# Small norm operations on GpSimd, and mixed channels loaded once for the second output projection

## The chip, the cores and the metric

The kernel runs on one core of a Trainium2 chip, as a single program. The metric is the time of one execution on the device in microseconds; of several runs the median is given. A profiled execution has its own time, which stands beside its span below.

The core has a matrix engine (TensorE, PE in the profile; PEld is its loading of weights), VectorE (DVE), ScalarE (ACT) and GpSimd (POOL). SyncE (SP) computes nothing here; most DMAs are issued from its queue. Each engine works through its own queue in order.

## The reference

One layer of a hybrid encoder on 2048 tokens of 1024 channels, then a final RMSNorm. Cut to what matters:

```python
h = rmsnorm(x, norm_mix_g)
u, dq, dk, dv, cq, cf, ci, cg = split_projection(h @ w_in)
y_a = s5_mixer(u, ...)                      # 256 channels
y_b = diff_attention(dq, dk, dv, ...)       # 6 heads x 64 channels
y_c = hgrn2_mixer(cq, cf, ci, cg, ...)      # 6 heads x 64 channels, the recurrence
x = x + concatenate([y_a, y_b, y_c]) @ w_out
h = rmsnorm(x, norm_ffn_g)
x = x + (gelu(causal_conv3(h @ w_up) + conv_b) * (h @ w_gate)) @ w_down
out = rmsnorm(x, final_norm_g)
```

Two of the norms matter here. In attention each head's output `o` (two softmax maps, subtracted and multiplied by `v`) goes through `rmsnorm(o, subln_g)` over its 64 channels. In the recurrence each head's `o` goes through `rmsnorm(o, norm_g)`, and is then multiplied by `silu(g)`. A norm needs, for every token and head, one reciprocal square root.

## The kernel before, in words

Products are made of f16 pairs: a float32 value is split into a high and a low half (`Ctx.split`, L52: ACT writes the high half at L55, DVE the low half at L61 or L63, or POOL at L59), and one product takes three matmuls. Tokens are tiled in four chunks of 512 (`CH`), channels in tiles of 128.

The program has two strands, `left` and `right` (L2050, L2061), that a function `weave` (L2084) interleaves by weights while the program is written down. The left strand projects to queries, keys and values and then runs attention in two passes: query blocks 0 to 7 for all six heads, then blocks 8 to 15. The right strand runs the S5 group, then the recurrence (`phase_hgrn`), then the tail (`phase_tail`). The order that each engine finally gets is made when the program is built: the context is opened with `schedule_with_timeline_sim=True` (L2131), so that a planner orders the instructions by a simulated time, and a change of one instruction's engine can move others.

**Attention's norms.** `phase_attn` (L754) collects, for each head `h` and pass, the sums of squares of its outputs in `H.ss` and the softmax sums in `H.la`, as tiles `[128, 8]` (128 tokens, 8 query blocks). When the last block of a head has been put away, `norm(h)` (L923) makes the factors: a reciprocal (L927), then on DVE two products (L928, L929), a scale with an added epsilon (L930), the reciprocal square root `K.rsqrt`, and a product (L934); POOL then multiplies the head's output by them (L935). After an odd head the pair is transposed by the PE (L944), split, and written to `Yd`, the mixed channels in DRAM (L948). There are 12 such norms.

**The reciprocal square root** (`Ctx.rsqrt`, L67): POOL raises to the power -0.5 (L72), and one step of Newton's method follows on DVE: L75, L84 and L85 for these two norms (n is 8).

**The recurrence's norms.** `phase_hgrn` (L1011) goes through 12 units (three pairs of heads by four chunks), each in the steps `proj`, `pre` and `fin`. In `fin` (L1290) ACT squares the output (L1335), DVE sums (L1337), scales and adds epsilon on DVE (L1340), calls `rsqrt` (L1343), lets POOL multiply by the gate (L1345), and multiplies on DVE by the factors (L1347).

**The output projection in two parts.** Chunks 0 and 1 are projected beside the recurrence (`early_mix`, L1375). Chunks 2 and 3 are projected in `second` (L1960) by `project` (L1467), between the down projection of the first MLP half and the second MLP half. `project` makes the columns in two halves `n`, and for each half goes through four groups `q` of 256 mixed channels. For each `n` and `q` it loads the mixed channels (`o_y`, two DMAs of 256 KB from `Yd`, L1478) and the weights in float32 (`o_wst`, 512 KB, L1480), splits the weights (`o_w`), and issues 24 matmuls (L1493). The channels do not depend on `n`, so they are loaded twice for each chunk. Their ring has 2 tiles, that of the split weights 3 and that of the raw weights 2 (L1967). `put` adds the product to the residual (`o_r`, L1506) and ACT makes sums of squares (`f_sq`, L1594). Between the two halves of chunk 3, chunk 2 is transposed for the MLP (`turned`, L1531). In the same stretch the last parts of the down projection run: raw weights `f_dst` are loaded (L1713) and combined on POOL and DVE (L1863), split into `f_dw`, and multiplied (`f_pd`, L1786); finished rows leave through L1608 and L1612.

Of the kernel before, what the change touches and what calls it, by code (L numbers as in the profile page):

```python
# [10 lines left out]
F16 = mybir.dt.float16  # L11
# [3 lines left out]
ALU = mybir.AluOpType  # L15
# [11 lines left out]
CH = 512  # L27
# [11 lines left out]
class Ctx:  # L39
# [24 lines left out]
                out=lo, in0=src, scalar=scale, in1=hi, op0=ALU.mult, op1=ALU.subtract  # L64
            )

    def rsqrt(self, pool, v, n, tag):  # L67

        nc = self.nc
        y = pool.tile([128, n], F32, tag=tag + "y", name="rs_y")  # L70
        t = pool.tile([128, n], F32, tag=tag + "t", name="rs_t")
        nc.gpsimd.tensor_tensor(  # L72
            out=y, in0=v, in1=self.mhalf.to_broadcast([128, n]), op=ALU.pow
        )
        nc.vector.scalar_tensor_tensor(  # L75
            out=t, in0=y, scalar=v[:, 0:1] if n == 1 else -0.5, in1=y, op0=ALU.mult, op1=ALU.mult
        )
        if n == 1:
            nc.vector.tensor_scalar(
                out=t, in0=t, scalar1=-0.5, scalar2=1.5, op0=ALU.mult, op1=ALU.add  # L80
            )
            nc.vector.tensor_tensor(out=y, in0=y, in1=t, op=ALU.mult)
        else:
            nc.vector.tensor_tensor(out=t, in0=t, in1=v, op=ALU.mult)  # L84
            nc.vector.scalar_tensor_tensor(  # L85
                out=y, in0=t, scalar=1.5, in1=y, op0=ALU.add, op1=ALU.mult
            )
        return y
# [665 lines left out]
def phase_attn(K, A, QKd, Vd, Yd, i0, i1, s_bufs, lean):  # L754
# [5 lines left out]
    tc, nc = K.tc, K.nc  # L760
    V = nc.vector
    NT = i1 - i0
    LM = 128 * i1
    base, nlam, lk, gc = A.base, A.nlam, A.lk, A.gc
    with ExitStack() as es:
        kp = es.enter_context(tc.tile_pool(name="t_k", bufs=2, reuse_waits="tile"))
        sp = es.enter_context(tc.tile_pool(name="t_s", bufs=s_bufs, reuse_waits="tile"))
        wp = es.enter_context(tc.tile_pool(name="t_w", bufs=2 if lean else 3, reuse_waits="tile"))
        mp = es.enter_context(tc.tile_pool(name="t_m", bufs=3, reuse_waits="tile"))
        op = es.enter_context(tc.tile_pool(name="t_o", bufs=2, reuse_waits="tile"))  # L770
# [152 lines left out]
        def norm(h):  # L923

            H = heads[h]
            s, v = [mp.tile([128, NT], F32, tag=f"e{j}", name=f"t_e{j}") for j in range(2)]
            V.reciprocal(out=s, in_=H.la[:, 0, :])  # L927
            V.tensor_tensor(out=v, in0=s, in1=s, op=ALU.mult)  # L928
            V.tensor_tensor(out=v, in0=v, in1=H.ss, op=ALU.mult)  # L929
            V.tensor_scalar(  # L930
                out=v, in0=v, scalar1=1.0 / HD, scalar2=EPS, op0=ALU.mult, op1=ALU.add
            )
            r = K.rsqrt(mp, v, NT, "rs")
            V.tensor_tensor(out=s, in0=s, in1=r, op=ALU.mult)  # L934
            nc.gpsimd.tensor_tensor(  # L935
                out=H.o, in0=H.o, in1=s.rearrange("p (t o) -> p t o", o=1).to_broadcast([128, NT, HD]),
                op=ALU.mult,
            )
            if h % 2 == 0:
                return  # L940
            for j in range(NT // 4):
                pt = ps_s.tile([128, 512], F32, tag="s", name="t_pt")
                for b in range(4):
                    nc.tensor.transpose(pt[:, 128 * b:128 * b + 128], H.y[:, 4 * j + b, :], K.ident)  # L944
                o = op.tile([128, 2, CH], F16, tag="yo", bufs=1, name="t_yo")
                K.split(o[:, 0, :], o[:, 1, :], pt, gc[:, 0:1])
                c0 = 128 * i0 + j * CH
                nc.sync.dma_start(out=Yd[2 + h // 2, :, :, c0:c0 + CH], in_=o)  # L948
            K.pairs.append(h // 2)
# [30 lines left out]
        for h in range(NH):  # L980
# [5 lines left out]
            for i in range(i0, i1):  # L986
# [10 lines left out]
                t = (h, i, [])  # L997
                n = 2 * (i // 4 + 1)
# [12 lines left out]
def phase_hgrn(K, Hd, w_in, lb_logits, norm_g, Yd, spare):  # L1011
# [5 lines left out]
    tc, nc = K.tc, K.nc  # L1017
    V = nc.vector
    C0 = 1408
    NB = CH // 128  # L1020
    with ExitStack() as es:
# [4 lines left out]
        wp = pool("g_w", 1)  # L1026
        st = pool("g_st", 1)
        hp = pool("g_h", 2)
        w3 = pool("g_3", 3)
        w2 = pool("g_2", 2)  # L1030
# [11 lines left out]
        for hl in (32, 16, 8):  # L1042
            m = ones[:, 0:64].rearrange("p (b y) -> p b y", y=hl)
            nb = 64 // hl
            t = w2.tile([128, nb, hl], F32, tag="d", name="g_mk")
# [11 lines left out]
        t = w2.tile([128, 16, 8], F32, tag="d", name="g_mk2")  # L1057
# [232 lines left out]
        def fin(u):  # L1290

            pr, j = divmod(u, NCH)
            vn, sg, qh, kt, eb, sc = ready.pop(u)
            po = [pp.tile([128, NB, HD], F32, tag="g", name=f"g_ps{a}") for a in range(2)]
            for bk in range(NB):
                for a in range(2):
                    rows = slice(64 * a, 64 * a + 64)
                    for e in range(2):
                        hh = slice(64 * e, 64 * e + 64)
                        nc.tensor.matmul(  # L1300
                            out=po[a][hh, bk, :], lhsT=kt[rows, bk, hh], rhs=vn[rows, bk, hh],
                            start=True, stop=True,
                        )
            sts = w2.tile([128, 2 * NB, HD], F32, tag="st", name="g_st")
            states = [state.get(u - 1, zero) if j else zero]
            for wn in range(2 * NB):
                last = 64 * wn + 63
                V.scalar_tensor_tensor(
                    out=sts[:, wn, :], in0=states[-1], scalar=eb[:, last:last + 1],
                    in1=po[wn % 2][:, wn // 2, :], op0=ALU.mult, op1=ALU.add,  # L1310
                )
                states.append(sts[:, wn, :])
            state[u] = states[-1]
            yield 1
            po = [pp.tile([128, NB, HD], F32, tag="g", name=f"g_po{e}") for e in range(2)]
            for bk in range(NB):
                for e in range(2):
                    nc.tensor.matmul(
                        out=po[e][:, bk, :], lhsT=sc[:, e, bk, :],
                        rhs=vn[:, bk, 64 * e:64 * e + 64], start=(bk == 0), stop=False,  # L1320
                    )
            for wn in range(2 * NB):
                bk, a = wn // 2, wn % 2
                for e in range(2):
                    hh = slice(64 * e, 64 * e + 64)
                    nc.tensor.matmul(
                        out=po[e][64 * a:64 * a + 64, bk, :], lhsT=qh[hh, 64 * wn:64 * wn + 64],
                        rhs=states[wn][hh, :], start=False, stop=(bk == NB - 1),
                    )
            sq = w2.tile([128, NB, 2, HD], F32, tag="d", name="g_sq")  # L1330
            y = w2.tile([128, NB, 2, HD], F32, tag="y", name="g_y")
            for e in range(2):
                nc.scalar.copy(y[:, :, e, :], po[e])
            yield 1
            nc.scalar.activation(out=sq, in_=y, func=AF.Square)  # L1335
            ss = w2.tile([128, 2 * NB], F32, tag="ss", name="g_ss")
            V.tensor_reduce(  # L1337
                out=ss, in_=sq.rearrange("p b e d -> p (b e) d"), axis=AX.X, op=ALU.add
            )
            V.tensor_scalar(  # L1340
                out=ss, in0=ss, scalar1=SQ * SQ / HD, scalar2=EPS, op0=ALU.mult, op1=ALU.add
            )
            r = K.rsqrt(w2, ss, 2 * NB, "rs")  # L1343
            yv = y.rearrange("p b e d -> p b (e d)")
            nc.gpsimd.tensor_tensor(out=yv, in0=yv, in1=sg, op=ALU.mult)  # L1345
            yb = y.rearrange("p b e d -> p (b e) d")
            V.tensor_tensor(  # L1347
                out=yb, in0=yb,
                in1=r.rearrange("p (t o) -> p t o", o=1).to_broadcast([128, 2 * NB, HD]),
                op=ALU.mult,  # L1350
            )
            yield 1
            pt = pp.tile([128, CH], F32, tag="g", name="g_py")
            for bk in range(NB):
                nc.tensor.transpose(pt[:, 128 * bk:128 * bk + 128], yv[:, bk, :], K.ident)
            o = w2.tile([128, 2, CH], F16, tag="d", name="g_yo")
            K.split(o[:, 0, :], o[:, 1, :], pt, gc[:, 0:1])
            nc.sync.dma_start(out=Yd[5 + pr, :, :, j * CH:(j + 1) * CH], in_=o)
            yield 1
# [67 lines left out]
def phase_tail(K, x, Xd, ss, Yd, Ad, w_out, norm_g, W, conv_w, conv_b, w_down, final_g, out, es,  # L1427
# [6 lines left out]
    V = nc.vector  # L1434
# [32 lines left out]
    def project(j, qs, st, wp, yp, pms, put, behind=None, between=()):  # L1467


        for n in range(2):  # L1470
            if n == 1:
                yield from between
            cc = slice(512 * n, 512 * n + 512)
            ps = [pms[n % len(pms)].tile([128, 512], F32, tag="m", name="o_pm") for t in range(4)]
            for q in qs:
                y = yp.tile([128, 2, 2, CH], F16, tag="y", name="o_y")
                for k in range(2):
                    nc.sync.dma_start(out=y[:, k], in_=Yd[2 * q + k, :, :, j * CH:(j + 1) * CH])  # L1478
                f = st.tile([128, 2, 512], F32, tag="wst", name="o_wst")
                d = nc.sync.dma_start(  # L1480
                    out=f, in_=w_out[0, 256 * q:256 * q + 256, cc].rearrange("(k p) f -> p k f", p=128)
# [478 lines left out]
    def second(pool, pm, before):  # L1960
# [3 lines left out]
        with ExitStack() as e3:  # L1964
            pool = pooler(e3)
            pm2 = pool("f_pm2", 4, space=PSUM)
            yp, wp, st = pool("o_y2", 2, "left"), pool("f_w2", 3, "left"), pool("f_st2", 2, "left")  # L1967
            fp, xp, rp = pool("f_f2", 2, "left"), pool("f_x", 1, "left"), pool("f_r4", 8, "left")
            left, right = sinks(hc, fp, 3, 2)
            r2, r3 = [], []  # L1970
# [164 lines left out]
```

## Time and profile before

| what | value |
|---|---|
| median of 3 runs | 2719.52 us (2718.45 to 2723.11) |
| the profiled execution's own time | 2723.9 us |
| its span in the profile | 2722.1 us |
| mean granted clock of the PE | 0.934 |
| bytes by DMA | 473.07 MB, 174 GB/s in the mean |

An engine's busy time is a sum over stages that have different limits, so it has to be read by stage. Attention's first pass lies beside S5's end and the recurrence, up to about 1080 us; its second pass lies beside the first MLP half and the start of that half's down projection, up to about 1920 us; the second output projection takes from about 1935 to 2073 us; the second MLP half and its down projection fill the rest. In the rows, `L96` means line 96, `A<-B` names the tile written and the tiles read, and `xN` counts instructions. The rings of tiles show as waits of the engine or queue that wants the next tile.

### The profile page before, as it was taken

The numbers are of one execution on the slowest core, as the hardware profiler recorded it, in microseconds if no ns is written. First come the engines' busy times: TensorE is split into PE (matmuls) and PEld (weight loads), VectorE is DVE, ScalarE is ACT, GpSimd is POOL, SyncE is SP. The second block draws the span as 40 slices with busy tenths as digits, with TensorE's granted clock in tenths as the row PEclk, the third lists the DMA queues.
The fourth block names the chain that finished last, engine by engine and source line by source line (L and its number), as shares of the span: only waits on it lengthen the run. The fifth ranks groups of instructions, "written<-read, shape, count | busy, mean of one in ns | idle before, by whom it ended". The sixth has DMA issues, their size and how long they took to land.

```text
span 2722.1 us, 42584 instructions
## 1 busy us (share of the span) xinstructions
PE 2408.0 (88%) x15438; PEld 1354.2 (50%) x15438; DVE 1873.5 (69%) x3401; ACT 1316.9 (48%) x2470; POOL 1350.7 (50%) x1149
## 2 busy tenths in 40 slices
PE   5998898888888889769988898598979999999998
PEld 4655556766766764334443444243434444444444
DVE  7467756688869885597788998865455655545565
ACT  6333344667757663564466766633235433333321
POOL 5688612455444542367677677515313344444280
PEclk8899898888989989879999999699989999999999
DMA  7676555467456666655466665688784655554733
GB/s 240 230 214 207 167 161 126 94 133 143 104 125 137 132 135 177 161 122 182 150 182 169 183 173 170 207 276 256 266 312 148 204 168 154 155 148 136 286 99 123
DMA packets 556740, 473.07 MB, mean 174 GB/s; under 512 B 277297, under 2 KB 433265, under 8 KB 555505
## 3 DMA queue, kind: packets, MB, share of 16 engines
q1 hardware_dynamic: 534352, 429.97, 56.0%
q10 hardware_dynamic: 22176, 40.38, 4.0%
q8 instruction: 121, 1.98, 0.3%
q14 instruction: 91, 0.74, 0.1%
HBM read 290.35 MB, written 125.83 MB: 153 GB/s over the span
## 4 chain that ended last, share of the span: by engine, by line
PE 22%; DVE 15%; issue 8%; POOL 7%; ACT 7%; DMA 6%; SPq 1%; ACTq 0%; DVEq 0%; POOLq 0%
PE f_pd L1786 10%; PE f_pm L96 7%; POOL f_k L1863 2%; DVE f_a L61 2%; DMA f_dst<-in_w_down_dram 2%; DVE t_sc L836 2%; DVE f_t L1617 2%; PE o_pm L1493 2%; PE o_pe L1411 2%; DVE t_sc L867 1%; DVE f_w L63 1%; POOL f_u L1863 1%; ACT f_t L1615 1%; ACT f_t L1910 1%; ACT t_sc L848 1%
## 5 line engine op out<-in xcount | busy, mean ns | idle before, releaser
L96 PE MATMUL f_pm<-f_q,f_w 128*128 128x512 f16 x3696 | 836.8, 386 | 30.0 <-DVE f_u L1863 9.2
L96 PEld LDWEIGHTS <-f_w 128*128 128x128 f16 x3696 | 363.3, 99 | 487.5 <-issue 70.1
L1786 PE MATMUL f_pd<-f_dw,f_da 128*128 128x512 f16 x1848 | 407.1, 382 | 2.7 <-DVE f_r L1764 1.5
L891 POOL TENSOR_TENSOR t_sc<-t_sc 128x1024 f16<-128x1024 f32 (+7 forms) x144 | 250.6, 1753 | 302.3 <-ACT t_sc L890 279.1
L1786 PEld LDWEIGHTS <-f_da 128*128 128x128 f16 x1848 | 181.1, 98 | 226.2 <-issue 14.5
L832 PE MATMUL t_ps<-t_k,t_q 96*128 96x512 f16 (+2 forms) x480 | 165.9, 372 | 94.6 <-DVE t_mx L836 80.2
L848 ACT ACTIVATE t_sc<-t_sc,t_nm 128x128 f32<-128x128 f32 (+7 forms) x192 | 230.5, 1201 | 6.6 <-DVE f_a L61 1.1
L836 DVE CUSTOM_DVE_ANT_0 t_sc<-t_ps,t_base,t_mx 128x512 f32<-128x512 f32 (+3 forms) x288 | 185.2, 643 | 18.9 <-PE t_ps L832 10.8
L61 DVE TENSOR_TENSOR f_a<-f_t,f_a 128x512 f16<-128x512 f32 x132 | 154.8, 1192 | 48.3 <-ACT f_a L55 47.8
L913 PEld LDWEIGHTS <-t_wt 128*128 128x128 f16 x2448 | 106.3, 101 | 121.3 <-DMA t_wt<-t_sc 50.4
L867 DVE SCALAR_TENSOR_TENSOR t_sc<-t_sc,t_a 128x1024 f32<-128x1024 f32 (+7 forms) x144 | 164.6, 1169 | 1.6
L96 PE MATMUL g_pq<-g_h,g_w 128*128 128x256 f16 x1152 | 159.2, 299 | 5.1 <-DVE g_sg L1160 2.7
L1863 POOL TENSOR_TENSOR f_t<-f_t,f_t 128x512 f32<-128x512 f32 x66 | 101.6, 1553 | 123.1 <-ACT f_a L55 108.8
L913 PE MATMUL t_po<-t_v,t_wt 128*128 128x64 f16 x2448 | 120.5, 198 | 47.2 <-DMA t_wt<-t_sc 42.4
L96 PE MATMUL g_pv<-g_w,g_h 128*128 128x256 f16 x1152 | 150.3, 288 | 9.2 <-ACT g_w L55 9.2
L1863 POOL TENSOR_TENSOR f_k<-f_k,f_k 128x512 f32<-128x512 f32 x88 | 124.5, 1414 | 51.5 <-ACT f_halo L1907 25.4
L1617 DVE SCALAR_TENSOR_TENSOR f_t<-f_u,f_cw,f_t 128x1024 f32<-128x1024 f32 x88 | 124.1, 1410 | 33.1 <-ACT f_t L1615 32.3
L836 DVE CUSTOM_DVE_ANT_0 t_sc<-t_ps,t_base 128x512 f32<-128x512 f32 (+2 forms) x192 | 120.4, 631 | 34.4 <-PE t_ps L832 13.7
L890 ACT CAST t_sc<-t_sc 128x1024 f16<-128x1024 f32 (+7 forms) x144 | 111.4, 792 | 64.4 <-DVE t_sc L867 63.4
L55 ACT ACTIVATE f_w<-f_sum 128x512 f16<-128x512 f32 x110 | 69.2, 629 | 146.4 <-DVE f_sum L139 62.2
L96 PEld LDWEIGHTS <-g_w 128*128 128x128 f16 x1152 | 121.3, 107 | 36.2 <-issue 6.4
L96 PEld LDWEIGHTS <-g_h 128*128 128x128 f16 x1152 | 116.8, 103 | 36.8 <-issue 10.8
(335 smaller groups left out, 4475.4 us busy)
## 6 DMA issues: line engine op xcount, KB each, us to landing
f_w<-Wd SPq DMA_DIRECT2D x231, 256.0 KB, 3.0
Wd<-f_w SPq DMA_DIRECT2D x154, 256.0 KB, 2.1
Ad<-f_a ACTq DMA_DIRECT2D x154, 256.0 KB, 2.7
f_da<-Ad SPq DMA_DIRECT2D x42, 768.0 KB, 4.9
g_h<-Hd SPq DMA_DIRECT2D x24, 1024.0 KB, 6.7
f_dst<-in_w_down_dram SPq DMA_DIRECT2D x48, 512.0 KB, 4.9
o_wst<-in_w_out_dram SPq DMA_DIRECT2D x24, 512.0 KB, 5.8
f_wst<-in_w_gate_dram SPq DMA_DIRECT2D x22, 512.0 KB, 5.6
```

Of the source, the lines that this page charges most:

```text
L61: nc.vector.tensor_tensor(out=lo, in0=src, in1=hi, op=ALU.subtract)
L96: nc.tensor.matmul(out=out, lhsT=lhs(a, k), rhs=rhs(b, k), start=(n == 0), stop=(n == 3 * nk - 1))
L832: nc.tensor.matmul(out=ps[:, 0:k1 - k0], lhsT=qt[:, c, 128 * (i % 4):128 * (i % 4) + 128], rhs=H.k[:, c, k0:k1], start=True, stop=True,)
L836: V.tensor_tensor_reduce(out=sc[c][:, k0:k1], in0=ps[:, 0:k1 - k0], in1=bs[:, k0:k1], scale=1.0, scalar=-3e38 if j == 0 else mx[:, c, j - ...
L848: nc.scalar.activation(out=sc[c][:, 0:L], in_=sc[c][:, 0:L], func=AF.Exp, scale=SLOPES[h], bias=nm[:, c:c + 1], accum_out=H.la[:, c, n_:n_ ...
L867: V.scalar_tensor_tensor(out=sc[0][:, k0:k1], in0=sc[1][:, k0:k1], scalar=a[:, 1:2], in1=sc[0][:, k0:k1], op0=ALU.mult, op1=ALU.add,)
L890: nc.scalar.copy(hl[:, k0:k1], sc[0][:, k0:k1])
L891: nc.gpsimd.tensor_tensor(out=hl[:, LM + k0:LM + k1], in0=sc[0][:, k0:k1], in1=hl[:, k0:k1], op=ALU.subtract,)
L913: nc.tensor.matmul(out=po, lhsT=wt[:, w, b, :], rhs=vt[:, b, 64 * v:64 * v + 64], start=(b == 0 and w + v == 0), stop=(b == i and w == 1),)
L1617: V.scalar_tensor_tensor(out=t0, in0=u[:, c:n + c], scalar=cw[:, c, m:m + 1], in1=t0, op0=ALU.mult, op1=ALU.add,)
L1786: nc.tensor.matmul(out=ps[t], lhsT=a[:, q, x, tk], rhs=w[:, y, q, :], start=(first and q + x + y == 0), stop=(last and q == n - 1 and y == 1),
L1863: eng.tensor_tensor(out=o, in0=a, in1=b, op=op)
```

## The change

`Ctx.rsqrt` gets a flag `aside`. With it, Newton's step is made on POOL by four instructions instead of three on DVE. Both norms use it, and their remaining small operations go to POOL as well: in attention's norm the two products, the scale and the last product (all but the reciprocal), in the recurrence's norm the scale. In `project` the mixed channels are loaded for the first half of the columns only and kept in a dictionary for the second half; their ring has 4 tiles instead of 2, and that of the split weights has 2 instead of 3. The other callers of `rsqrt` keep DVE.

```diff
-    def rsqrt(self, pool, v, n, tag):
+    def rsqrt(self, pool, v, n, tag, aside=False):
...
         nc.gpsimd.tensor_tensor(
             out=y, in0=v, in1=self.mhalf.to_broadcast([128, n]), op=ALU.pow
         )
+        if aside:
+            nc.gpsimd.tensor_tensor(out=t, in0=y, in1=y, op=ALU.mult)
+            nc.gpsimd.tensor_tensor(out=t, in0=t, in1=v, op=ALU.mult)
+            nc.gpsimd.tensor_scalar(
+                out=t, in0=t, scalar1=-0.5, scalar2=1.5, op0=ALU.mult, op1=ALU.add
+            )
+            nc.gpsimd.tensor_tensor(out=y, in0=y, in1=t, op=ALU.mult)
+            return y
...
             V.reciprocal(out=s, in_=H.la[:, 0, :])
-            V.tensor_tensor(out=v, in0=s, in1=s, op=ALU.mult)
-            V.tensor_tensor(out=v, in0=v, in1=H.ss, op=ALU.mult)
-            V.tensor_scalar(
+            P = nc.gpsimd
+            P.tensor_tensor(out=v, in0=s, in1=s, op=ALU.mult)
+            P.tensor_tensor(out=v, in0=v, in1=H.ss, op=ALU.mult)
+            P.tensor_scalar(
                 out=v, in0=v, scalar1=1.0 / HD, scalar2=EPS, op0=ALU.mult, op1=ALU.add
             )
-            r = K.rsqrt(mp, v, NT, "rs")
-            V.tensor_tensor(out=s, in0=s, in1=r, op=ALU.mult)
+            r = K.rsqrt(mp, v, NT, "rs", True)
+            P.tensor_tensor(out=s, in0=s, in1=r, op=ALU.mult)
...
-            V.tensor_scalar(
+            nc.gpsimd.tensor_scalar(
                 out=ss, in0=ss, scalar1=SQ * SQ / HD, scalar2=EPS, op0=ALU.mult, op1=ALU.add
             )
-            r = K.rsqrt(w2, ss, 2 * NB, "rs")
+            r = K.rsqrt(w2, ss, 2 * NB, "rs", True)
...
+        ys = {}
         for n in range(2):
...
             for q in qs:
-                y = yp.tile([128, 2, 2, CH], F16, tag="y", name="o_y")
-                for k in range(2):
-                    nc.sync.dma_start(out=y[:, k], in_=Yd[2 * q + k, :, :, j * CH:(j + 1) * CH])
+                if n == 0:
+                    y = yp.tile([128, 2, 2, CH], F16, tag="y", name="o_y")
+                    for k in range(2):
+                        nc.sync.dma_start(
+                            out=y[:, k], in_=Yd[2 * q + k, :, :, j * CH:(j + 1) * CH])
+                    ys[q] = y
+                y = ys[q]
...
-            yp, wp, st = pool("o_y2", 2, "left"), pool("f_w2", 3, "left"), pool("f_st2", 2, "left")
+            yp, wp, st = pool("o_y2", 4, "left"), pool("f_w2", 2, "left"), pool("f_st2", 2, "left")
```

## The prediction

> **What bounds the kernel now.** I read the page first, then the busy time by stages, the waits of the PE, and last, for the two places that are edited, the timeline and the groups of instructions.
>
> ```profile
> span 2722.1 us, 42584 instructions
> PE 2408.0 (88%) x15438; PEld 1354.2 (50%) x15438; DVE 1873.5 (69%) x3401; ACT 1316.9 (48%) x2470; POOL 1350.7 (50%) x1149
> ```
>
> ```profile
> 480.00:1080.00 600.00, 527.71 (x5363) 404.26 (x5363) 479.19 (x1223) 382.12 (x883) 273.03 (x226) 0.91 0.60 131
> 1110.00:1760.00 650.00, 534.75 (x3080) 254.15 (x3079) 541.41 (x841) 396.06 (x673) 430.83 (x275) 0.90 0.59 169
> 1978.00:2051.00 73.00, 56.05 (x232) 23.38 (x232) 37.53 (x60) 28.64 (x54) 11.61 (x10) 0.88 0.83 297
> 2110.00:2722.00 612.00, 601.41 (x2772) 271.53 (x2771) 336.83 (x394) 192.38 (x301) 258.53 (x172) 0.99 0.52 164
> ```
>
> The columns are the stretch, its length, busy time (instructions) of PE, PEld, DVE, ACT and POOL, the granted clock, the DMA share and GB/s. Attention beside the recurrence (480 to 1080) leaves the PE idle for 72.3 us, with DVE at 80% and POOL at 46%. Attention beside the first MLP half (1110 to 1760) has DVE at 83% and POOL at 66%. The second output projection (1978 to 2051) holds only 56.05 us of PE work in 73, at a clock of 0.88, with the DMA at 83%. After 2110 the PE is 98% busy, and no line of the change runs there: time won ahead of 2110 should reach the end whole.
>
> ```profile
> PE t_ps L832 <- DVE t_mx L836: 80.2, 63, 7.3
> PE t_po L913 <- DMA t_wt<-t_sc: 42.4, 25, 6.6
> PE o_pm L1493 <- DMA o_y<-Yd: 16.9, 6, 7.6
> ```
>
> ```profile
> PE t_ps L832 <- DVE t_mx L836: 11.4, 16, 1.8
> ```
>
> Each row gives who waits for whom, microseconds in total, times, longest. The first fence is the whole span, the second the stretch 480 to 1110 alone. Both edits have a target here: the projection's PE waits for `o_y`, which the change loads half as often, and attention's PE waits for DVE, which the change relieves. But of those 80.2 us, only 11.4 lie beside the recurrence, where most of the norms are.
>
> **The change: mixed channels loaded once.** Of 32 loads of `o_y`, the 16 of the second column half go (256 KB each, 4 MB). The ring grows from 2 tiles to 4, so a chunk's four tiles can be asked for before any is used up; the `o_w` ring shrinks from 3 to 2. The PE in this stage:
>
> ```profile
> 1971.53 6.64 PE L1493 MATMUL o_pm<-o_w,o_y 128*128 128x512 f16 x30
> 1981.46 12.22 PE L1493 MATMUL o_pm<-o_w,o_y 128*128 128x512 f16 x48 [3.30 <-DMA o_y<-Yd]
> 2001.32 7.91 PE L1493 MATMUL o_pm<-o_w,o_y 128*128 128x512 f16 x24 [7.64 <-DMA o_y<-Yd]
> 2017.01 10.53 PE L1493 MATMUL o_pm<-o_w,o_y 128*128 128x512 f16 x48 [1.21 <-DMA o_y<-Yd]
> 2036.44 14.16 PE L1493 MATMUL o_pm<-o_w,o_y 128*128 128x512 f16 x57 [2.46 <-DMA o_y<-Yd]
> ```
>
> One `q` is 24 matmuls. At the clean rate (10.53/48 = 0.219 us) it takes 5.26 us. Two losses go with the loads. First, the waits: 16.9 us by the row above. Second, the slow matmuls behind a wait: 48 took 12.22 instead of 10.53 (1.7 lost), 24 took 7.91 instead of 5.26 (2.65), 57 took 14.16 instead of 12.5 (1.7); together 6.0. At most 22.9 us can go. The stage says the same: 232 matmuls at 0.219 are 50.8 us, 22.2 below its 73. The clock shows why: 0.88 in the stage, after waits of 2.46 us and more.
>
> The Trainium skill, "TensorE: Matmul & The Clock Gate", "What's actually happening", says that an idle window of about 3.4 us halves the PE clock, and about 3.4 us of work restores it. The trace agrees on the 7.64 us gap, but 2.46 and 3.30 us also cost 1.7 us each here. By the page's window alone the sum would be 3.4 us smaller; the rows decide.
>
> What is late next? For a `q` it is its weights: a load, ACT's high half, DVE's low half.
>
> ```profile
> L55 ACT ACTIVATE o_w<-o_wst x16: 1039/1048/1057, 1934.5 to 2057.1; 128x1024 f16<-128x1024 f32 x16
> L63 DVE SCALAR_TENSOR_TENSOR o_w<-o_wst,o_w x16: 1211/1226/2285, 1936.5 to 2058.2; 128x1024 f16<-128x1024 f32 x16
> ```
>
> ```profile
> o_wst<-in_w_out_dram SPq DMA_DIRECT2D x10, 512.0 KB, 7.3
> o_r<-in_x_dram SPq DMA_DIRECT2D x8, 512.0 KB, 8.7
> out_dram<-f_r SPq DMA_DIRECT2D x4, 512.0 KB, 9.9
> ```
>
> ```profile
> 1978.00:1990.00 12.00, 8.70 (x33) 3.55 (x33) 12.00 (x21) 8.82 (x19) 6.36 (x5) 0.86 0.41 132
> ```
>
> ```profile
> 1986.83 1.21 DVE L63 SCALAR_TENSOR_TENSOR o_w<-o_wst,o_w 128x1024 f16<-128x1024 f32 x1
> ```
>
> The second fence is median microseconds to landing in 1978 to 2051. Two staging tiles alternate, so a `q` costs half of load plus splits: (7.3 + 1.05 + 1.23)/2 = 4.8 us, just below 5.26. With the slower landing of `o_r`, 8.7, it is 5.5: 0.24 too much for each of the some 9 `q` in the stretch, 2 us; I take half of that, 1 us, since the queue moves fewer bytes than now. Two `o_w` tiles instead of three cost nothing as long as a split (2.3 us) fits under the next `q` (5.26). That cover fails once: between 1978 and 1990 DVE is busy for 12.00 of 12.00 us with the ends of the down projection. The fourth `q` would now end at 1978.17 + 5.26 = 1983.4 (1978.17 is the end of the first row), but the next `q`'s low half is done only at 1988.0 in DVE's present order. That leaves a gap of 4.6 us and, behind it, 1.7 of slow matmuls: 6.3.
>
> SP's queue runs in order. The early loads of the third and fourth `q` (four issues) must stand behind the last write of attention's channels and may be put ahead of `f_dst` loads, on which the down projection hangs. A queue place there costs 0.6 us (median issue, row below), so 0 to 2.4 us. I take 0.6, as the PE then has projection matmuls to fill with.
>
> ```profile
> L1478 SPq DMA_DIRECT2D o_y<-Yd x32: 517/600/1247, 1904.8 to 2063.1; - x32
> ```
>
> Sum: 22.9 - 6.3 - 1.0 - 0.6 = **15 us gained**. Ends: 22.9 if DVE's order adapts; 8 if every landing takes as long as that of `out`, (9.9 + 2.3)/2 = 6.1, which is 0.84 too much nine times (7.6), with the other losses.
>
> **The change: norms on GpSimd.** An attention norm gives up 7 DVE instructions (L928, L929, L930, three of Newton's step, L934), a recurrence norm 4 (L1340 and three). There are 12 of each: 132 instructions. Their groups between 480 and 1930:
>
> ```profile
> L75 DVE SCALAR_TENSOR_TENSOR rs_t<-rs_y 128x8 f32<-128x8 f32 x24 | 14.5, 604 | 5.0 <-POOL rs_y L72 4.9
> L85 DVE SCALAR_TENSOR_TENSOR rs_y<-rs_t,rs_y 128x8 f32<-128x8 f32 x24 | 7.7, 320 | 0.4
> L934 DVE TENSOR_TENSOR t_e<-t_e,rs_y 128x8 f32<-128x8 f32 x12 | 4.6, 380 | 0.2
> L1340 DVE TENSOR_SCALAR g_ss<-g_ss 128x8 f32<-128x8 f32 x12 | 4.4, 366 | 0.1
> L928 DVE TENSOR_TENSOR t_e<-t_e 128x8 f32<-128x8 f32 x12 | 4.0, 332 | 0.2
> L929 DVE TENSOR_TENSOR t_e<-t_e,t_ss 128x8 f32<-128x8 f32 x12 | 3.5, 291 | 12.9 <-ACT t_sq L877 12.9
> L930 DVE TENSOR_SCALAR t_e<-t_e 128x8 f32<-128x8 f32 x12 | 2.9, 240 | 0.2
> L84 DVE TENSOR_TENSOR rs_t<-rs_t,t_e 128x8 f32<-128x8 f32 x12 | 2.6, 214 | 0.1
> L84 DVE TENSOR_TENSOR rs_t<-rs_t,g_ss 128x8 f32<-128x8 f32 x12 | 2.1, 178 | 0.2
> ```
>
> After the bar: busy time, mean ns, idle time just before. DVE is rid of 46.3 us of work, and of 17.9 us in which it stood at L75 and L929 waiting for POOL or ACT. Twenty of the 24 norms lie before 1110 (all 12 of the recurrence and 8 of attention): 20/24 of 46.3, 38.6 us, is 8% of DVE's 479 there. The PE's direct waits for attention's maximum in that stage are 11.4 us, so 8% of all PE idleness there, 72.3, is a generous 6 us. I take 4 for both attention stages.
>
> POOL gains 8 instructions for each attention norm and 5 for each recurrence norm: 156. It has small ones already, in the S5 phase:
>
> ```profile
> L583 POOL TENSOR_TENSOR s_tb<-s_ct,s_col 128x8 f32<-128x8 f32 x4 | 2.3, 586 | 0.0
> L579 POOL TENSOR_TENSOR s_ct<-s_tb,s_tb 128x8 f32<-128x8 f32 x4 | 1.2, 290 | 0.3
> ```
>
> ```profile
> L72 POOL TENSOR_TENSOR rs_y<-g_ss,mhalf x12: 1637/1643/1890, 509.8 to 1065.9; 128x8 f32<-128x8 f32 x12
> L1347 DVE TENSOR_TENSOR g_y<-g_y,rs_y x12: 678/691/1914, 513.2 to 1069.5; 128x512 f32<-128x512 f32 x12
> L1345 POOL TENSOR_TENSOR g_y<-g_y,g_sg 128x512 f32<-128x512 f32 x12 | 16.0, 1335 | 36.6 <-ACT g_sq L1335 36.6
> ```
>
> I take 0.3 us (L579 has the contiguous tiles that the norms have): 47 us more on POOL, 91 by L583. At 46% busy it has the room. What counts is its queue, which runs in order: behind an attention norm stand `t_sc`'s low halves (L891), whose transposes the PE waits for, and behind a recurrence norm stands DVE itself at L1347. That chain is now 3.4 us from the power to L1347 (509.8 to 513.2). Then it is the new scale at the head, power, four small ones and the product with `g_sg`, if that stays last: 0.3 + 1.64 + 1.2 + 1.34 = 4.5 us, 1.1 more, 12 times 13 us, during which DVE stands still if its order has L1347 that early. Its own work there shrinks by 17.6 us (L1340's 4.4, L84's 2.1, half of L75's 14.5 and of L85's 7.7). I charge 2 us for both queues. Sum: **2 us gained**, with ends of 12 (the freed waits of 17.9 also reach the PE in part) and a loss, below.
>
> Together 17 us. The profiled execution took 2723.9 us, 1.8 outside its span; it becomes 2707. It stands 4.4 above the median of 2719.5, so the median becomes **2702.5**.
>
> **Rivals.** *The weights take the place of the channels.* For it: 4.8 against 5.26 us is thin, the DMA is at 83%, and `o_w` loses a tile. Against it: the removed loads stood in the same queue. If landings stay at 10 us and DVE's backlog costs 6.3 twice, only 2 to 4 of the 22.9 are left, and with 1 from the norms: 2715.
>
> *The norms on POOL become the wait (slower).* The shared rows show small instructions stretched: L75 took 604 ns in the mean where L84 took 178. If POOL's small ones are stretched alike to 0.8 us, a recurrence norm's chain is 5 x 0.8 + 1.64 + 1.34 = 7.0, 3.6 more than now; 12 of them hold DVE at L1347 for 43 us, less the 17.6 given back: 25 us lost, if all of it shows, against 15 gained: 2730. It decides from a mean of about 0.63 us on: 5 x 0.63 + 2.98 - 3.4 = 2.7, 12 times 33, less 17.6, is the projection's whole gain. Against it: POOL's rows of 0.29 us, and the recurrence's output is wanted late. The Trainium skill, "GPSIMD Engine Reference", section "Engine selection", speaks for this rival: it gives elementwise work to VectorE, GpSimd being about twice as slow for two inputs. The trace agrees: 0.29 us on POOL (L579) against 0.178 on DVE (L84).
>
> *The relief counts more.* DVE's order closes up in attention and in the projection: 22.9 and 9 gained: 2688.
>
> **How the numbers follow.** Forecast 0.58, weights 0.18, slower norms 0.14, more relief 0.10. About 0.2% (5.4 us, below 2714.1 or above 2725) is what a measurement can tell. Faster: 0.58 + 0.10 + 0.04 of the weights' case, which straddles the bound, is 0.72. Within: the other 0.14 and 0.01 of the norms' case, 0.15. Slower: 0.13. The range takes in the forecast, the weights' case and half of the relief: 2689 to 2719, leaving out 0.14 and 0.05. The forecast's own range is 2694 to 2711.
>
> **What would show it.** Right: 16 issues of `o_y`; no PE wait for them past 1 us; the stage from the first to the last projection matmul some 15 us shorter, at a clock above 0.95; 156 POOL instructions on 128x8 near 0.3 us; DVE some 46 us less busy; 612 us from the start of the second MLP half to the end, as before. Wrong: PE waiting for ACT or DVE `o_w`, or for `f_dw`, as long as it did for `o_y`; POOL's small ones above 0.6 us with DVE idle at L1347; or a shift before 2110 that the last stage takes back.

## The result, and the profile after

The changed kernel takes 2745.33 us in the median of 4 runs (2738.93 to 2749.52), beside 2720.12 us for the kernel before (2718.45 to 2723.11). The ratio is 1.0096, with a 95% interval of 1.0077 to 1.0115: 26 us slower, where 17 us faster was forecast. The profiled execution took 2747.4 us.

The head of the page after, to be set beside the two lines that open the prediction:

```profile
span 2745.7 us, 42512 instructions
PE 2437.3 (89%) x15438; PEld 1372.5 (50%) x15438; DVE 1845.0 (67%) x3269; ACT 1317.0 (48%) x2470; POOL 1389.3 (51%) x1305
```

As intended, VectorE has 132 instructions fewer and GpSimd 156 more. VectorE is 28.5 us less busy, not 46.3. The surprise is the PE: the same 15438 matmuls keep it busy 29.3 us longer.

Busy time by stages, first of the kernel before, then of the one after (columns as in the prediction). The bounds are events: 440 us is about where attention's first products with the values start, the next bound is the start of the first MLP half, then come the first and the last matmul of the second output projection, and the last 612 us.

```profile
440.00:1180.90 740.90, 637.79 (x6207) 474.56 (x6206) 564.13 (x1427) 463.12 (x1046) 316.75 (x263) 0.90 0.60 132
1180.90:1935.60 754.70, 650.85 (x3691) 303.73 (x3691) 591.84 (x882) 408.23 (x681) 458.33 (x283) 0.92 0.64 191
1935.60:2073.00 137.40, 120.29 (x541) 54.12 (x541) 76.00 (x96) 51.77 (x90) 36.19 (x22) 0.94 0.74 260
```

```profile
440.00:1210.20 770.20, 665.14 (x6223) 493.46 (x6224) 542.91 (x1328) 462.02 (x1042) 347.15 (x385) 0.87 0.58 129
1210.20:1971.00 760.80, 653.22 (x3649) 301.86 (x3649) 579.25 (x847) 405.56 (x675) 462.95 (x312) 0.92 0.63 190
1971.00:2095.70 124.70, 115.11 (x532) 53.16 (x532) 74.47 (x94) 52.20 (x91) 37.08 (x22) 0.97 0.67 242
2133.70:2745.70 612.00, 598.30 (x2751) 269.26 (x2749) 335.42 (x392) 191.78 (x300) 258.01 (x171) 0.99 0.51 164
```

The projection is 12.7 us shorter, at a clock of 0.97. The last 612 us are as they were. The loss is 29.3 us in the first row, attention beside the recurrence, and 6.1 us in the second. In the first row the PE's idle time hardly differs (740.90 - 637.79 = 103.1 us before, 105.1 after); its busy time grows by 27.4 us for the same work, and the granted clock falls from 0.90 to 0.87. So in this stage the time went to a slower clock, not to longer waits.

The waits of the PE after, over the whole span:

```profile
PE t_ps L841 <- DVE t_mx L845: 88.1, 68, 7.3
PE t_po L922 <- DMA t_wt<-t_sc: 43.1, 29, 8.0
...
PE o_pm L1509 <- ACT o_w L55: 8.9, 4, 4.7
```

The wait for `o_y` is gone. Attention's two waits, which the relief of VectorE should have shortened, were 80.2 and 42.4 us and are 88.1 and 43.1.

Four of the ten groups of GpSimd's new instructions (after the bar: busy time, mean ns, idle time before), and the wait that the recorded rival named:

```profile
L77 POOL TENSOR_TENSOR rs_t<-rs_y 128x8 f32<-128x8 f32 x24 | 7.5, 312 | 0.9
L82 POOL TENSOR_TENSOR rs_y<-rs_y,rs_t 128x8 f32<-128x8 f32 x24 | 7.0, 292 | 1.4
L940 POOL TENSOR_SCALAR t_e<-t_e 128x8 f32<-128x8 f32 x12 | 5.4, 447 | 1.1
L1350 POOL TENSOR_SCALAR g_ss<-g_ss 128x8 f32<-128x8 f32 x12 | 2.4, 204 | 1.0
```

```profile
DVE g_y L1357 <- POOL rs_y L82: 9.7, 4, 4.8
```

The ten groups together are 156 instructions and 47.9 us, 0.307 us each. VectorE stands at L1357 (L1347 before) for 9.7 us in the recurrence. Neither the prices nor this wait explain 26 us.

### The profile page after: what moved, and what is told of

It reads as the page before. It is cut to its first block, busy times and chain, and to the rows that moved or that the text cites. A ratio compares the mean times of both kernels' runs of the same rounds, so it can differ in the third digit from the quotient of the medians.

```text
span 2745.7 us, 42512 instructions
## 1 busy us (share of the span) xinstructions
PE 2437.3 (89%) x15438; PEld 1372.5 (50%) x15438; DVE 1845.0 (67%) x3269; ACT 1317.0 (48%) x2470; POOL 1389.3 (51%) x1305
## 5 line engine op out<-in xcount | busy, mean ns | idle before, releaser
L841 PE MATMUL t_ps<-t_k,t_q 96*128 96x512 f16 (+2 forms) x480 | 166.4, 379 | 103.3 <-DVE t_mx L845 88.1
L876 DVE SCALAR_TENSOR_TENSOR t_sc<-t_sc,t_a 128x1024 f32<-128x1024 f32 (+7 forms) x144 | 175.3, 1243 | 1.9
L105 PE MATMUL g_pv<-g_w,g_h 128*128 128x256 f16 x1152 | 161.2, 299 | 11.5 <-ACT g_w L55 8.5
L922 PE MATMUL t_po<-t_v,t_wt 128*128 128x64 f16 x2448 | 122.5, 201 | 47.7 <-DMA t_wt<-t_sc 43.1
L105 PE MATMUL g_pq<-g_h,g_w 128*128 128x256 f16 x1152 | 151.4, 289 | 2.9 <-ACT g_w L55 0.9
L55 ACT ACTIVATE f_a<-f_t 128x512 f16<-128x512 f32 x154 | 95.0, 627 | 82.0 <-POOL f_t L1879 33.8
```

Source lines behind the costliest of these rows:

```text
L55: nc.scalar.activation(out=hi, in_=src, func=AF.Copy, scale=scale)
L105: nc.tensor.matmul(out=out, lhsT=lhs(a, k), rhs=rhs(b, k), start=(n == 0), stop=(n == 3 * nk - 1))
L841: nc.tensor.matmul(out=ps[:, 0:k1 - k0], lhsT=qt[:, c, 128 * (i % 4):128 * (i % 4) + 128], rhs=H.k[:, c, k0:k1], start=True, stop=True,)
L876: V.scalar_tensor_tensor(out=sc[0][:, k0:k1], in0=sc[1][:, k0:k1], scalar=a[:, 1:2], in1=sc[0][:, k0:k1], op0=ALU.mult, op1=ALU.add,)
L922: nc.tensor.matmul(out=po, lhsT=wt[:, w, b, :], rhs=vt[:, b, 64 * v:64 * v + 64], start=(b == 0 and w + v == 0), stop=(b == i and w == 1),)
```

## The experiments

All ratios are to the kernel before, run on the same chip in the same session; "us" is the ratio times 2720. Where an expectation gives a figure of an earlier run, it is that run's ratio or difference of medians, which are up to 3 us apart.

| kernel | what it is | ratio [95%] | us |
|---|---|---|---|
| after | the change | 1.0096 [1.0077, 1.0115] | +26.1 |
| e1_proj | projection half alone | 0.9951 [0.9935, 0.9967] | -13.3 |
| e2_norms | both norms on GpSimd alone | 1.0132 [1.0116, 1.0149] | +35.9 |
| e3_attn | attention's norms alone | 1.0052 [1.0037, 1.0067] | +14.1 |
| e4_rec | the recurrence's norms alone | 1.0093 [1.0075, 1.0111] | +25.3 |
| c1_scale | the recurrence's scale alone | 1.0040 [1.0026, 1.0053] | +10.9 |
| n1_memset | before, one idle memset | 1.0005 [0.9990, 1.0020] | +1.4 |
| n2_memset | before, two idle memsets | 1.0002 [0.9988, 1.0016] | +0.5 |
| m1_memset | e2_norms, one idle memset | 1.0137 [1.0116, 1.0157] | +37.3 |
| p1_norms_old_order | e2_norms in the order of before | 1.0002 [0.9989, 1.0016] | +0.5 |
| p2_before_new_order | before in the order of e2_norms | 1.0148 [1.0129, 1.0166] | +40.3 |
| p3_after_e1_order | the change in the order of e1_proj | 0.9959 [0.9943, 0.9976] | -11.2 |
| q1_pe_old | e2_norms, TensorE in the old order | 1.0039 [1.0023, 1.0054] | +10.6 |
| q2_rest_old | e2_norms, the other four in the old order | 1.0062 [1.0045, 1.0079] | +16.9 |
| s3_pe_dve_old | e2_norms, TensorE and VectorE in the old order | 1.0048 [1.0028, 1.0068] | +13.1 |
| r1_load_old_order | before plus 156 idle operations, old order | 1.0018 [1.0007, 1.0030] | +4.9 |
| r2_relief_old_order | before without Newton's steps, old order | 0.9988 [0.9976, 1.0000] | -3.3 |
| s1_load_free | r1's program, planner's order | 1.0045 [1.0027, 1.0063] | +12.2 |
| s2_relief_free | r2's program, planner's order | 1.0055 [1.0034, 1.0076] | +15.0 |

**The change taken apart.** e1_proj undoes both norms, e2_norms the projection, e3_attn and e4_rec the projection and one of the norms:

```diff
 e1_proj, of both norms:
-            r = K.rsqrt(w2, ss, 2 * NB, "rs", True)
+            r = K.rsqrt(w2, ss, 2 * NB, "rs")
...
 e2_norms, e3_attn, e4_rec, in project and where its rings are made:
-                if n == 0:
+                if True:
...
-            yp, wp, st = pool("o_y2", 4, "left"), pool("f_w2", 2, "left"), pool("f_st2", 2, "left")
+            yp, wp, st = pool("o_y2", 2, "left"), pool("f_w2", 3, "left"), pool("f_st2", 2, "left")
```

> Only the projection's half of the change: channels loaded once, rings 4 and 2, norms on DVE as before. In the changed kernel the stretch from the first to the last projection matmul shrank from 136.9 to 124.2 us while everything before it was 35 us late. Theory A (the norms lost it, the projection won): 2704 to 2711 us, 9 to 16 below the kernel before, all of it gained after 1930. Rival B (the two halves hinder each other, or the gain is only the planner's luck in the changed kernel): no faster than 2717.

> Only the norms' half of the change: all small operations of both norms on GpSimd, projection as before. Theory A: the loss of the changed kernel plus the projection's gain, 2753 to 2762 us, with the delay built up between 440 and 1180. Rival B: the norms cost less than 30 us, 2735 to 2749.

> Only attention's 12 norms on GpSimd (96 of its 156 new instructions). If the work on GpSimd and its in-order queue are the cost, the loss of the norms divides about by instructions: some 20 us lost here, 2738 to 2745, and this loss and that of the next kernel add up to that of both norms together within 6 us. If it is the order that the planner makes of a changed program, the parts need not add up, and this kernel lies anywhere from 2710 to 2760.

> Only the recurrence's 12 norms on GpSimd (60 of the 156 instructions). By the work and the queue: some 15 us lost, 2732 to 2738, adding up with the kernel before this one. By the recorded rival, DVE held at the product with the factors for longer, the loss sits in that line's idle time: above 15 us there. By the planner's order: anywhere from 2710 to 2760, and no sum.

The projection half gains 13.3 us, as the forecast's first term (15). The norms lose 35.9 us, and nearly additively: 14.1 + 25.3 = 39.4. The stage that holds the projection in e1_proj:

```profile
1930.10:2057.20 127.10, 117.61 (x532) 53.70 (x532) 76.33 (x95) 51.47 (x90) 38.97 (x22) 0.95 0.66 238
```

**Chance of the order, first try.** Another idea was that the planner's order changes with any edit and that the loss is chance. n1_memset and n2_memset add idle work to the kernel before, m1_memset adds it to e2_norms, and c1_scale moves one group of 12 operations:

```diff
 n1_memset (n2_memset has one more in the first unit of the recurrence):
         zero = cp.tile([128, HD], F32, name="g_zero")
         nc.gpsimd.memset(zero, 0.0)
+        idle = cp.tile([128, 1], F32, name="g_idle")
+        nc.gpsimd.memset(idle, 0.0)
...
 c1_scale, the kernel before with:
-            V.tensor_scalar(
+            nc.gpsimd.tensor_scalar(
                 out=ss, in0=ss, scalar1=SQ * SQ / HD, scalar2=EPS, op0=ALU.mult, op1=ALU.add
```

> The kernel before with one more GpSimd memset of 128x1 (some 0.1 us) on a tile that nothing reads, at the head of the recurrence. The work is the same, but the planner gives some 890 of DVE's 3209 instructions another place in the order. Theory of work and queues (the norms' operations on GpSimd cost the 37 us): 2715 to 2726, as before. Rival, the order (a changed program gets another order, and the order sets how long the PE stays at half clock between 440 and 1165): off by 6 us or more, in either direction.

> The same with a second such memset in the first unit of the recurrence; some 500 DVE instructions change places against the kernel with one. Work and queues: 2715 to 2726. Order: off by 6 us or more, and not by the same amount as with one memset.

> The kernel with both norms on GpSimd and the projection as before, with the one memset of 128x1 at the head of the recurrence. Work and queues: 2752 to 2762 like the kernel without it (2757). Order: 6 us or more away from that, and if the norms on GpSimd cost nothing by themselves, within the spread of the kernels with norms on DVE.

> The kernel before with only the recurrence's scale (one small instruction for each of 12 norms) moved from DVE to GpSimd; the planner moves some 680 DVE instructions. Work and queues: 12 of the 60 instructions of the recurrence's share, 25 us for all, so 2 to 6 us slower, 2722 to 2727. Order: anywhere from 2700 to 2745, and as likely outside 2715 to 2730 as inside.

The memsets changed nothing, and I took that as proof that the order does not matter. That was a misreading. The lists of the programs' instructions do differ in some 890 lines on VectorE, but only in the numbers of their buffers. Compared by place, none of TensorE's, VectorE's, ScalarE's or SyncE's instructions stands elsewhere than in the kernel without the memset. These runs show how well two equal programs repeat (0.05%), and nothing about the order. c1_scale, with 12 operations of about 0.2 us moved, does reorder: in its trace 1465 of TensorE's 15438 matmuls leave the order that it has in common with the kernel before, up to 592 places away, and it loses 10.9 us. In e2_norms it is 1957 of them, or 1687 of the 14414 instructions that the program gives TensorE.

**The order held.** So that operations and order can be varied one at a time, a chain of edges was added on each engine. Such an edge orders the issue of two neighbours on one engine and adds no wait:

```diff
     with tile.TileContext(nc, schedule_with_timeline_sim=True) as tc:
         tile_trunk_kernel(tc, *args)
+        pin(tc, nc)
...
+def pin(tc, nc):
...
+            if last is not None:
+                tc.add_manual_dep(
+                    ins[at], last.name,
+                    mybir.DependencyInfo(mybir.DependencyClass.NoSync, mybir.DependencyReason.DATA),
+                    reason="order",
+                )
+            last = ins[at]
```

`ORDER`, which `pin` goes through, holds for each engine the places that the planner gave the instructions in another kernel. In p1 VectorE's 132 operations are simply missing from that list, and GpSimd's 156 are put right next to their power, which is my placing and not the planner's. In p2 VectorE's 132 stand where the plan of e2_norms issues GpSimd's. The traces bear the orders out: the matmuls of p1 stand as in the kernel before, those of p2 as in e2_norms, all 15438.

> Both norms on GpSimd, the projection as before; the order of the instructions on every engine is held to that of the kernel before, by edges between neighbours that order the issue and add no wait. Only the 132 operations are gone from VectorE's order, and GpSimd's 156 stand next to their power. Work theory (GpSimd's small operations and their longer chain cost the time by themselves): 25 to 40 us slower than before, as with the planner's own order (+36.6). Order theory (the loss is in the order that the planner makes once these operations are GpSimd's): within 6 us of before, or a few us faster, since VectorE is relieved.

> The operations of the kernel before, all on their old engines, but every engine held to the order of the kernel with both norms on GpSimd; VectorE's 132 operations stand where that plan issues GpSimd's. Work theory: within 6 us of before. Order theory: 25 to 40 us slower than before, though nothing is on GpSimd that was not there.

> The whole change, each engine held to the order of the kernel with the projection half alone (e1_proj, 12.5 us faster than before). Work theory: 20 to 30 us slower than before, as the change is. Order theory: 6 to 18 us faster than before.

All three fall to the order theory. With the old order the moved norms cost 0.5 us (-3.0 to 4.4). With the new order and no operation moved the kernel loses 40.3 us. The whole change, held to e1_proj's order, is 11.2 us faster than before. The first stage, of p1 and then of p2:

```profile
440.00:1170.10 730.10, 631.69 (x6181) 471.33 (x6179) 535.65 (x1322) 461.75 (x1043) 350.57 (x386) 0.90 0.59 134
```

```profile
440.00:1214.90 774.90, 664.82 (x6222) 492.93 (x6223) 572.37 (x1432) 462.53 (x1039) 315.44 (x259) 0.87 0.57 128
```

The clock and the PE's busy time go with the order, not with the operations: 631.69 us at 0.90 in the old order, with the norms on GpSimd; 664.82 us at 0.87 in the new one, with the norms on VectorE. Between the two rows lie 44.8 us: 33.1 are busy time and 11.7 idle (98.4 against 110.1). GpSimd's wait of the rival's kind is there in p1 too, in the recurrence, without harm:

```profile
DVE g_y L1357 <- POOL rs_y L82: 7.0, 4, 2.7
```

**Which engine's order.** Some engines held to the old order, the others left to the planner, with the norms on GpSimd:

```diff
 pin goes through, of ORDER:
+q1_pe_old      PE
+q2_rest_old    DVE, Activation, Pool, SP
+s3_pe_dve_old  PE, DVE
```

> Both norms on GpSimd, projection as before; TensorE alone held to its order of the kernel before, the other engines in the order that the planner then makes (it moves 131 of VectorE's instructions against before, by 11 places at most). If TensorE's order carries the loss: within 6 us of before. If VectorE's or ScalarE's order carries it: more than 10 us slower.

> The reverse: VectorE, ScalarE, GpSimd and SyncE held to the order of before, TensorE as the planner orders it (526 of its 14414 instructions stand elsewhere than before, against 1687 in the planner's free order). If TensorE's order carries the loss, in that share: 5 to 20 us slower than before. If the others carry it: within 6 us of before.

> Both norms on GpSimd, projection as before; TensorE and VectorE held to the order of before, the other three as the planner then orders them (55 of ScalarE's 2200 instructions and 11 of GpSimd's stand elsewhere, by 4 places at most). If VectorE's order was what q1_pe_old lacked: within 5 us of before. If ScalarE's and GpSimd's few places matter: 5 to 12 us slower.

Neither theory fits: q1 (10.6 us) recovers about two thirds of the 35.9 and q2 (16.9 us) about one half, and holding VectorE as well brings nothing more (13.1 us). These are not the two halves of e2_norms' order: with some engines held, the planner orders the rest anew, and in q2 it moves 526 of TensorE's instructions instead of 1687. q2 differs from p1 in TensorE's order alone, so that order by itself can cost 16.9 us; q1 shows that time is lost with TensorE's order kept, too. In s3 only ScalarE, GpSimd and SyncE differ from p1; of the instructions that the kernel before has, 55 of ScalarE's and 11 of GpSimd's stand elsewhere, by 4 places at most. What stands out in its profile is GpSimd's queue in the first stage. s3's waits of GpSimd and, for L1357, of VectorE:

```profile
POOL t_e L938 <- DVE t_e L936: 16.3, 5, 4.7
```

```profile
DVE g_y L1357 <- POOL rs_y L82: 12.0, 6, 2.9
```

The planner sets L938, the first of an attention norm's small products, where GpSimd stands 16.3 us for VectorE's reciprocal; p1 has no such wait. And it puts other work between a power and its Newton step, and L1357 waits 12.0 us instead of 7.0. That these waits make the 13 us is not shown. The kernel before has a wait of GpSimd for VectorE in the same norms:

```profile
POOL rs_y L72 <- DVE t_e L930: 22.2, 6, 6.1
```

And e2_norms, which loses 35.9 us, stands 15.4 us at L938, no longer than s3 does. ScalarE's 55 moved instructions may share in the loss; that was not taken apart.

**The two terms, each by itself.** r1 adds only GpSimd's load, r2 takes only VectorE's (Newton's steps of these norms are left out, so its norms have the accuracy of the bare power), both with the order held; s1 and s2 are the same two programs as the planner orders them.

```diff
 r1, s1, in rsqrt behind the power (8 times for attention's norms, 5 for the recurrence's):
+            for _ in range(aside):
+                nc.gpsimd.tensor_tensor(out=z, in0=v, in1=v, op=ALU.mult)
...
 r2, s2, in rsqrt behind the power, for these norms:
+        if aside is None:
+            return y
```

> The kernel before with its order held on every engine, and 156 more 128x8 products on GpSimd behind the norms' powers (8 for an attention norm, 5 for one of the recurrence), into a tile that nobody reads; VectorE keeps its operations. GpSimd's longer queue by itself: by the prediction's term 2 us slower (0 to 5). If the zero of p1_norms_old_order is two larger terms that cancel: 6 us or more slower.

> The kernel before with its order held, and the Newton step of both norms left out (72 of the 132 operations on VectorE, nothing added anywhere; its norms are the bare power's). VectorE's relief by itself: by the prediction's term some 2 us faster (4 us for all 132). If larger terms cancel: 6 us or more faster. If VectorE's small operations are hidden: no change within 3 us.

> The same program as r1_load_old_order (156 idle products on GpSimd, nothing taken from VectorE), in the order that the planner makes of it. If the old order is one that any replanning spoils: 10 to 40 us slower than before, against 4.9 with the order held. If only the move off VectorE spoils it: 3 to 8 us slower, as with the order held.

> The same program as r2_relief_old_order (both norms' Newton step left out, nothing added), in the order that the planner makes of it. If any replanning spoils the order: 10 to 40 us slower than before, though it has less to do. If only work added to GpSimd spoils it: 0 to 6 us faster, as with the order held.

With the order held, load costs 4.9 us (1.9 to 8.2) and relief of 72 operations gives 3.3 (0 to 6.5): small terms that cancel, as p1 says. In the planner's own order both programs are slower, even s2, which has 72 instructions fewer than the kernel before and nothing added: 15.0 us slower, 18.3 from its twin. Its first stage:

```profile
440.00:1190.10 750.10, 643.92 (x6231) 481.54 (x6229) 557.06 (x1369) 461.39 (x1042) 316.80 (x260) 0.89 0.59 131
```

So it is not the move to GpSimd that the planner answers badly. All six programs here that alter the norms' operations alone and were planned afresh (c1, e3, e4, e2, s1, s2; m1 is e2 once more) are 10.9 to 35.9 us slower than before. The order of the kernel before is one that the planner did not find again in any of them. e1_proj, planned afresh with the norms untouched, nearly keeps it: by its trace, 34 of the 15438 matmuls leave it.

The fastest kernels are e1_proj (2708.28 us) and the whole change in e1_proj's order (2707.74 us, of another session). Their ratios to before, 0.9951 and 0.9959, overlap: with a good order the norms' place makes no difference that can be measured.

## Why the prediction was wrong

*Projection, 15 us gained: right in its mechanism, and 13.3 (9.0 to 17.7) takes in its size.* The 16 issues are there, no PE wait for `o_y` is left, the clock is 0.97, and the stage is 12.7 us shorter (10.3 in e1_proj).

```profile
L1491 SPq DMA_DIRECT2D o_y<-Yd x16: 518/528/1167, 1937.3 to 2051.1; - x16
```

The one term seen to be too small is the backlog of split weights. It was put at 6.3 us and at VectorE's door; the PE now waits 8.9 us for `o_w`, put down to ScalarE's half, the longest wait being 4.7 us where 4.6 was worked out. The weights did not take the place of the channels beyond that.

*GpSimd's operations, 156 at 0.3 us: right.* 47.9 us against 47. They were hardly slower than on VectorE: 0.307 us in the mean against 46.3/132 = 0.35, 0.202 in the median against 0.167. The recorded 0.29 against 0.178 set a short group of GpSimd's beside VectorE's shortest. The rival of stretched operations (0.8 us each, 43 us of VectorE standing at L1347) ends on the side that came true, but its mechanism did not occur: 0.307 us each, 9.7 us of standing, and 7.0 us of it in a kernel that loses nothing. A result on a rival's side does not confirm the rival.

*Relief 4 us, queues 2 us, sum 2 us gained: about right in the order for which they were worked out.* Load alone measured 4.9, relief of 72 of the 132 operations 3.3, both together 0.5 lost (3.0 gained to 4.4 lost). The 2 us charged for both queues lie just inside the interval of the 4.9 (1.9 to 8.2).

*VectorE some 46 us less busy: wrong.* It is 28.5 over the span, and 37.4 in p1, where the old order is kept (1836.1 against 1873.5). The 46.3 was a sum of means that a few long operations pull up, as mean and median above show. And two kernels with the same 3401 operations on VectorE as before, e1_proj and r1, have 1881.3 and 1867.3 us, so differences of this size also come without a change of VectorE's work. What lengthens single operations was not followed.

*The step that failed is under all of these.* Every norm term was priced at a place in the old order ("if its order has L1347 that early", "if that stays last"), and the only reordering considered was a good one ("DVE's order closes up"). But this kernel's order is planned anew with each edit, from times that a planner assumes; the description of the kernel says so, and the sum still put the price of a new order at nothing. The move of 156 small instructions made the planner set 1687 of TensorE's 14414 elsewhere. That has a price of its own, 40.3 us with no operation moved, twenty times the 2 us that the terms came to, and no rival had it. Nor did any of the signs named under "Wrong" appear: the loss came mostly as a slower clock in the stage of attention beside the recurrence, and the prediction counted the clock in the projection alone. The change as measured is then the sum of e1_proj and e2_norms, -13.3 + 35.9 = 22.6, against 26.1.

*Where the new order loses* can be read from the first stage by taking off its length the PE's idle time and the time lost to the clock. The latter is (1 - clock) times the length, added up over windows of 2 us: 75.4 us before, 72.1 in p1, 104.0 after, 104.5 in p2. Lengths less both are 740.9 - 103.1 - 75.4 = 562.4, then 559.6, 561.1 and 560.3: about the same work each time. Of p2's 34.0 us beyond the kernel before, 29.1 are clock and 7.0 idle, and the rest is 2.1 shorter. These are single executions: n1_memset and n2_memset, with the order of the kernel before, have 731.3 and 733.9 us in this stage, of which 76.4 and 70.6 are clock, so some 10 us of length and 6 of clock can differ without any change of order.

*What stays open.* Why that order lets the clock fall more often is not settled. The PE's gaps in the first stage are more and smaller in p2 (of more than 0.15 us: 83 gaps with 101.6 us before, 96 with 107.8 in p2), but their number alone does not tell: n2_memset has 90 and loses nothing, s2 has 76 and e4_rec 85, and both are slow. No run changed the gaps alone. Nor was it tried what in the planner's assumed times makes it choose so.

## What to carry to other kernels

Where a planner sets the order, an edit has two prices: that of its operations, which a profile can give, and that of the new order, which it can't; here the second was the larger by far. Hold the order and change the operations, then hold the operations and change the order, before a part of an edit is believed or dropped, and keep a good order when an edit costs it. A control for "only the order changed" must be compared place by place, or it may be the same program.

## What the runs showed of the hardware

How much a gap of the PE costs behind its end. p2 around 895 us, the PE's work and, below, the stretches of 2 us (column 8 is the granted clock):

```profile
892.39 0.41 PE L922 MATMUL t_po<-t_v,t_wt 128*128 128x64 f16 x8 [1.27 <-DMA t_wt<-t_sc]
893.91 1.11 PE L922 MATMUL t_po<-t_v,t_wt 128*128 128x64 f16 x32 [1.11 <-DMA t_wt<-t_sc]
898.20 1.12 PE L841 MATMUL t_ps<-t_k,t_q 96*128 96x512 f16 x3 [3.18 <-DMA t_k<-QKd]
```

```profile
894.00:896.00 2.00, 1.02 (x32) 0.90 (x32) 2.00 (x3) 0.78 (x1) 0.79 (x1) 1.00 1.07 240
896.00:898.00 2.00, 0.00 (x0) 0.00 (x0) 0.85 (x2) 0.00 (x0) 1.25 (x1) 0.67 0.89 184
898.00:900.00 2.00, 1.80 (x11) 1.28 (x12) 0.70 (x2) 0.38 (x3) 0.86 (x1) 0.50 0.00 0
900.00:902.00 2.00, 2.00 (x19) 1.67 (x17) 0.75 (x1) 1.52 (x3) 0.00 (x0) 0.50 0.00 0
902.00:904.00 2.00, 2.00 (x12) 1.40 (x11) 1.57 (x5) 0.56 (x2) 1.49 (x2) 0.50 0.32 64
904.00:906.00 2.00, 2.00 (x12) 1.44 (x10) 1.87 (x3) 1.97 (x4) 2.00 (x2) 0.50 1.13 227
906.00:908.00 2.00, 2.00 (x15) 1.52 (x14) 0.59 (x2) 0.31 (x2) 0.83 (x1) 0.77 0.89 214
```

The PE works from 898.20 on, and fully from 900, yet the clock stays at half until about 907, some 9 us. At half clock that is over 4 us of work lost behind a wait of 3.18 us, and the table of waits shows only the wait. Such stretches of half clock last 3.4 us or a whole multiple of it (3.4, 6.8, 10.2, 13.7 and 17.1 us, worked out from windows of half a microsecond). From 440 us to the first MLP half there are 24 of them with 151 us before, 23 with 144 us in p1, 32 with 209 us in p2 and 30 with 208 us after.

The Trainium skill, "TensorE: Matmul & The Clock Gate", "What's actually happening", puts such a window at about 3.4 us and has it run freely. The multiples agree. It names one idle window as the cause and 3.4 us of sustained work as the cure. In the rows above no gap reaches 3.4 us, and the first nearly full 3.4 us behind it did not restore the clock.
